# RWKV-7 outputs accumulated channel-major from head-centred values, with the group norm's variance from block-ones products

## The chip, the cores and the metric

The kernel runs on one NeuronCore of a Trainium2 chip. The metric is device time in microseconds (us) of one execution, lower is better; the median of three timed runs stands for the kernel. The profile is of one more execution of the same program.

## The reference, cut to what matters

The model is a two-layer decoder trunk over 1024 tokens of width 1024. The change touches only the RWKV-7 branch of the first layer, which has 16 heads of 64 channels. After its recurrence each head's output is normalised over the head's 64 channels, a bonus is added, and the result is gated and given to the output projection:

```python
def step(state, inp):
    r_t, w_t, k_t, v_t, kk_t, b_t = inp
    sa = -jnp.einsum('bhij,bhj->bhi', state, kk_t)
    state = (state * w_t[:, :, None, :] + sa[..., None] * b_t[:, :, None, :]
             + v_t[..., None] * k_t[:, :, None, :])
    return state, jnp.einsum('bhij,bhj->bhi', state, r_t)
...
mean = jnp.mean(y, -1, keepdims=True)
var = jnp.mean(jnp.square(y - mean), -1, keepdims=True)
y = ((y - mean) * lax.rsqrt(var + RW_GN_EPS)).astype(p.dtype).reshape(b, s, h * n) * ln_w + ln_b
bonus = jnp.sum(r * k * r_k, -1, keepdims=True) * v
return y + bonus.reshape(b, s, h * n)
```

The state's row index is the value's channel, and every term that enters y is linear in v. If v is centred over a head's 64 channels, y comes out centred over them too, so the mean over the head is zero and the variance is the mean of y squared.

## The kernel before

TensorE never runs a stage alone. One long chain of dense products (the projections; rows `mm<-xhi,wh`, `mm<-xlo,wh`, `mm<-xhi,wl` in the trace, three per 128x512 product of exact parts) runs in the background, and the stages are streams (Python generators) with a higher rank. The class `Flow` sets TensorE's order when the program is built: it keeps a planned time, a stream yields what its next step waits for (a planned time, PSUM buffers, an event), and the first ready stream in rank emits its next products; the background chain fills the rest. That order is fixed on TensorE. The order on VectorE, ScalarE and GpSimd comes from the tile framework's own schedule; each of them works strictly in its queue's order.

The RWKV stage lies between about 60 and 1090 us of the span. Its work is cut into 16 units: 8 head pairs times two halves of 512 tokens, each unit four chunks of 128 tokens. Per unit:

- `rw_prep0`, `rw_prep1`: channel-wise work (128 channels = two heads on partitions, 512 tokens). `rw_prep1` transposes V, B and K to token-major (`tok`, by TensorE, copied by ScalarE) and makes the masked products `gr`.
- `rw_inv0`, `rw_inv1`: inverses of triangular blocks. `rw_inv0` has a chain of 62 dependent small operations on GpSimd (L710 and L712, tiles `titmp` and `ti`) with transfers before and after.
- `rw_seq`: the four chunks in turn. Two such streams (of two head pairs) run interleaved. Within a chunk: `rp` and `sp` products, `up` products that give the next state (VectorE, L827, tile `s0c`), and last the outputs, five products into the bank `yps`.
- `rw_out`: group norm, bonus, gate, result to DRAM. Its first part runs when a unit's `rw_seq` has ended; it then yields 10 planned us; its second part begins with four transposes on TensorE.

Before the change the outputs are token-major, and `rw_out` does this: VectorE sums y over each head (L841), subtracts the mean (L844), ScalarE squares (L847), VectorE sums the squares (L848) and finds the inverse root by Newton's method in 15 operations on 128x8 elements (`rsqrt`, L869 to L877, tile `gmv`); **GpSimd multiplies y by it (L850, tile `ty`)**; TensorE transposes `ty` to channel-major (`g<-ident,ty`); VectorE applies weight and bias (L858), adds the bonus (L861) and gates (L862). The five output products of a chunk are these, all in fp32, which the trace shows as two records per product:

```python
F.matmul(yp[:, b, :], lhsT=kr[:, b, 1, :], rhs=sc, start=True, stop=False)
for h, hs in enumerate(hsl):
    F.matmul(yp[:, b, hs], lhsT=gb[:, h, 1, :], rhs=tok[:, 0, b, hs], start=False, stop=False)
    F.matmul(yp[:, b, hs], lhsT=gr[:, b, h, :], rhs=sa[:, h, :], start=False, stop=(h == 1))
```

L179 is the one line through which all matmuls go and L183 the one for transposes, so groups are told apart by their tiles. L404 and L405 split a tile into two exact parts, `hi` by ScalarE and `lo` by VectorE. `head_sums` multiplies two such parts by `blk`, a matrix of ones on the two 64x64 diagonal blocks.

Of the kernel before, what the change touches and what calls it, by code (L numbers as in the profile page):

```python
# [29 lines left out]
# ---------------------------------------------------------------- host layout  # L30
# [24 lines left out]
def host_arrays(inp):  # L55
# [5 lines left out]
    # the S5 channels of a tile: by channel in the group, then by group  # L61
# [26 lines left out]
    # rows 32 r + q, column 2 c + i: channel q of group 2 r + i of tile c  # L88
# [23 lines left out]
    # by head pair, for both halves of the rows  # L112
# [46 lines left out]
class Flow:  # L159
    """The order of TensorE's work. Streams (generators) share it: the first one in rank that is  # L160
    ready goes on by a step. A stream yields what its next step waits for: a time in us from now,
    a PSUM tag and a number of its buffers, the name of an event, or a list of these."""
# [8 lines left out]
    # TensorE, in the order of the calls  # L171
# [13 lines left out]
    # PSUM buffers  # L185
# [11 lines left out]
    # events  # L197
# [27 lines left out]
    def run(self, until):  # L225
        """until the given streams have ended"""
# [19 lines left out]
class Item:  # L246
    """One product of the dense chain: out[m, tokens] = w^T x as three products of exact parts.
    x(h): (hi, lo) [128, kt, 512]; evac(h, psum) takes a half of the tokens. gen: any other work instead"""
# [8 lines left out]
class Tiles(list):  # L257
    """tiles [128, n], indexed as one [128, k, n] would be"""
# [6 lines left out]
class K:  # L265
# [4 lines left out]
    # ------------------------------------------------------------ constants  # L270
    def consts(self, es):
# [22 lines left out]
        # 1 - mu  # L294
# [10 lines left out]
    def new_banks(self, g, yps):  # L305
        """banks besides the dense chain's two"""
# [13 lines left out]
    # ------------------------------------------------------------ dense  # L320
    def load_w(self, parts, src, kt, m=P, pool=None):
        """generator: exact parts of a weight tile [128, kt, m], in pieces; yields the end of each"""
# [14 lines left out]
    def dense(self, items):  # L337
        """generator: the chain of dense products, the weights of the next ones loaded ahead"""
# [17 lines left out]
        def fill(n):  # L356
            """weights of the items up to the next but one, as far as there is room"""
            while at[0] < min(n, len(items) - 1) or live[0] < WB and at[0] < min(n + 2, len(items) - 1):
                at[0] = next(todo)
# [42 lines left out]
    def split(self, hi, lo, src):  # L402
        """hi + lo = src exactly, each with float32r's significand"""
        self.nc.scalar.copy(hi, src)  # L404
        self.nc.vector.tensor_tensor(lo, src, hi.bitcast(F32), A.subtract)  # L405

    def split_load(self, pool, hi, lo, src, n=HT):
        """exact parts of a DRAM tile [128, T]"""
# [5 lines left out]
    def gate2(self, g, ps):  # L414
        """g = 2 * silu(ps)"""
# [4 lines left out]
    def keep_evac(self, kind, dst):  # L420
        """evac of a projection to DRAM: 'gate', 'u' or 'copy'"""
        nc = self.nc

        def evac(h, ps):
            t = self.wp.tile([P, HT], F32, name="ev", bufs=2)
            if kind == "u":
                # tokens by place in the block, last first
# [11 lines left out]
    def put_y(self, kt, s, y):  # L439
        """y [128, n]: out-projection input kt, to DRAM"""  # L440
        self.nc.sync.dma_start(self.yd[kt, :, s], y)

    # ------------------------------------------------------------ norms
    def rstd(self, r, n, fill, scale_mat, rank_wait=0):
        """generator: r [128, n] = (mean over channels + eps)^-1/2 on every partition;
        fill(i, s): squares of one part of the channels for tokens s, or None after the last"""
# [14 lines left out]
    def norm_first(self, p, h, xhi, xlo):  # L461
        """generator: half of the input's tokens as exact parts, first without their norm (a factor per token, self.r0)
        for the products that come first, then with it"""
# [42 lines left out]
    def rw_consts(self, p):  # L506
# [10 lines left out]
        nc.vector.memset(self.p5, 0.5)  # L517
        self.blk = p.tile([P, P], F32R, name="blk")
# [4 lines left out]
        # per channel: w0 / 2, a0 / 2, 1 - k_a  # L523
# [6 lines left out]
        # identity start of the 32-row triangular inverses, in 4 interleaved column groups  # L530
        self.t0 = p.tile([P, 8, 32], F32, name="t0")
        nc.gpsimd.memset(self.t0, 0.0)
        for q in range(4):
            # t - 4 cc - q != 0 keeps 0, else 1
# [1940 lines left out]
```

## Time and profile before

| | |
|---|---|
| timed runs | 2821.52, 2826.01, 2829.27 us; median 2826.01 |
| profiled execution, first to last instruction | 2839.6 us (its time outside the span is not reported) |
| TensorE matmul busy | 2604.9 us, 92% of the span |
| VectorE / ScalarE / GpSimd busy | 1787.5 / 1250.4 / 807.9 us |
| mean granted TensorE clock | 0.944 of 2.4 GHz |

A busy share is an average over stages that have different limits. In this kernel TensorE's order is fixed, so time is lost where TensorE stands idle or runs at the lower clock, and the view that says why is the list of what its instructions waited for. "idle before ... <-" in a row names the idle time of that engine just before the instruction and what ended it.

### The profile page before, as it was taken

The page shows a single profiled execution, that of the slowest core. Times are in us where ns is not written, and L with a number is a line of the kernel's source. Part 1 is how long each engine was busy: PE and PEld are TensorE (multiplying, and loading weights), DVE is VectorE, ACT ScalarE, POOL GpSimd, SP SyncE. Part 2 cuts the span into 40 slices and gives each one's busy share as a digit, 9 for nine tenths or more (in the row PEclk, how much of TensorE's full clock was granted, in tenths as well). Part 3 has the DMA queues.
Part 4 walks back from the last instruction along what each step waited for, and adds up shares of the span by engine and source line. Part 5 has one row for each costly group of instructions (what it writes and reads, how often), then busy time and mean ns, then how long its engine had stood idle before and what let it go on. Part 6 is the DMA issues. An engine that isn't in the chain of part 4 may idle for free.

```text
span 2839.6 us, 42364 instructions
## 1 busy us (share of the span) xinstructions
PE 2604.9 (92%) x15058; PEld 2058.7 (72%) x15058; DVE 1787.5 (63%) x3383; ACT 1250.4 (44%) x2446; POOL 807.9 (28%) x1507
## 2 busy tenths in 40 slices
PE   7998899998998998888999998989899989999998
PEld 5776777776777776675678776767787767777786
DVE  8755556665655537787656457877734887776532
ACT  7433334333443333545533346435434445555443
POOL 4433544345435403354200111251420120000011
PEclk9998989999999989987999999999999999999999
DMA  4332223333232243454584564242455231113643
GB/s 156 115 100 77 84 77 90 95 86 93 85 100 68 70 127 134 107 162 150 160 274 137 162 189 122 79 107 77 113 163 190 88 103 62 44 45 98 197 134 100
DMA packets 263860, 328.27 MB, mean 116 GB/s; under 512 B 88017, under 2 KB 135249, under 8 KB 263137
## 3 DMA queue, kind: packets, MB, share of 16 engines
q1 hardware_dynamic: 260736, 319.39, 37.1%
q0 software_dynamic: 1280, 4.20, 0.4%
q8 instruction: 119, 1.95, 0.3%
q10 hardware_dynamic: 1632, 1.98, 0.2%
q14 instruction: 93, 0.75, 0.1%
HBM read 232.59 MB, written 92.90 MB: 115 GB/s over the span
## 4 chain that ended last, share of the span: by engine, by line
PE 50%; DMA 16%; DVE 15%; POOL 8%; issue 5%; ACT 4%; SPq 1%; DVEq 0%; ACTq 0%; POOLq 0%
PE mm L179 32%; PE g L179 12%; DMA ai<-d_in 5%; PE yps L179 3%; POOL ti L712 3%; POOL titmp L710 3%; PE g L183 2%; DVE wl L405 2%; DMA lm<-acd 1%; DMA gsz<-zd 1%; DMA w<-in_w_ev_out 1%; DMA d_in<-ga 1%; DMA spl<-yg 1%; DMA y<-yt 1%; DMA spl<-yd 1%
## 5 line engine op out<-in xcount | busy, mean ns | idle before, releaser
L405 DVE TENSOR_TENSOR wl<-w,wh 128x512 fp32r<-128x512 f32 (+2 forms) x410 | 285.0, 699 | 295.5 <-ACT wh L404 288.4
L404 ACT CAST wh<-w 128x512 fp32r<-128x512 f32 (+2 forms) x410 | 241.9, 594 | 429.4 <-PE mm L179 274.3
L179 PE MATMUL mm<-xhi,wh 128*128 128x512 f32 x832 | 371.0, 446 | 25.5 <-DVE ev L418 13.7
L179 PE MATMUL mm<-xlo,wh 128*128 128x512 f32 x832 | 344.2, 414 | 4.7 <-DVE xlo L496 2.4
L179 PE MATMUL mm<-xhi,wl 128*128 128x512 f32 x832 | 343.1, 412 | 0.0
L179 PE MATMUL mm<-x1h,wh 128*128 128x512 f32 (+1 forms) x608 | 254.4, 418 | 25.1 <-ACT craw L1822 14.3
L179 PE MATMUL mm<-x1h,wl 128*128 128x512 f32 (+1 forms) x608 | 243.4, 400 | 0.0
L179 PE MATMUL mm<-x1l,wh 128*128 128x512 f32 (+1 forms) x608 | 243.1, 400 | 0.0
L710 POOL TENSOR_TENSOR titmp<-ai,ti 128x60 f32<-128x60 f32 (+24 forms) x496 | 151.3, 305 | 313.8 <-DMA ai<-d_in 277.1
L179 PEld LDWEIGHTS mm<-xhi,wh 128*128 128x128 f32 x832 | 165.6, 199 | 82.7 <-issue 24.2
L179 PEld LDWEIGHTS mm<-xhi,wl 128*128 128x128 f32 x832 | 165.4, 199 | 40.5
L179 PEld LDWEIGHTS mm<-xlo,wh 128*128 128x128 f32 x832 | 166.6, 200 | 36.2 <-DVE xlo L474 5.0
L712 POOL TENSOR_TENSOR ti<-ti,titmp 128x60 f32<-128x60 f32 (+24 forms) x496 | 161.2, 325 | 38.2
L179 PEld LDWEIGHTS mm<-x1h,wh 128*128 128x128 f32 (+1 forms) x608 | 117.9, 194 | 59.0 <-ACT craw L1822 17.3
L179 PEld LDWEIGHTS mm<-x1l,wh 128*128 128x128 f32 (+1 forms) x608 | 117.6, 193 | 27.6 <-issue 3.6
L179 PEld LDWEIGHTS mm<-x1h,wl 128*128 128x128 f32 (+1 forms) x608 | 117.2, 193 | 27.0
L179 PE MATMUL mm<-yb,wh 128*128 128x512 f32 x320 | 102.4, 400 | 5.8 <-ACT yb L404 4.5
L785 DVE TENSOR_TENSOR gb<-g,m 128x256 f32<-128x256 f32 x128 | 49.5, 419 | 73.2 <-PE g L179 73.0
L799 ACT ACTIVATE sn<-s0c,fin 64x64 f32<-64x64 f32 x128 | 44.1, 345 | 106.4 <-DVE s0c L827 57.8
L1673 POOL TENSOR_TENSOR sq<-sq,sqt 128x512 f32<-128x512 f32 x14 | 18.0, 1289 | 245.7 <-DMA w<-in_w_ev_out 161.0
L2266 POOL CAST pth<-zero 128x128 fp32r<-128x128 f32 x32 | 11.3, 353 | 241.4 <-PE yps L179 179.8
L418 DVE SCALAR_TENSOR_TENSOR ev<-ev,mm 128x512 f32<-128x512 f32 x72 | 49.1, 682 | 45.5 <-ACT ev L417 45.2
(598 smaller groups left out, 6612.7 us busy)
## 6 DMA issues: line engine op xcount, KB each, us to landing
w<-in_w_ev_in SPq DMA_DIRECT2D x106, 256.0 KB
w<-in_w_od_in SPq DMA_DIRECT2D x82, 256.0 KB
w<-in_w_ev_out SPq DMA_DIRECT2D x64, 256.0 KB
w<-in_w_od_out SPq DMA_DIRECT2D x64, 256.0 KB
rd<-ev SPq DMA_DIRECT2D x50, 256.0 KB
spl<-yd SPq DMA_DIRECT2D x40, 256.0 KB
zod<-ev SPq DMA_DIRECT2D x36, 256.0 KB
ai<-d_in SPq DMA_DIRECT2D x16, 512.0 KB
```

What stands on the lines that cost most here:

```text
L179: return self._pe(self.nc.tensor.matmul(out, lhsT=lhsT, rhs=rhs, start=start, stop=stop, **kw), math.prod(rhs.shape[1:]), rhs.dtype)
L183: return self._pe(self.nc.tensor.transpose(out, src, ident), src.shape[0] // 2, F32)
L404: self.nc.scalar.copy(hi, src)
L405: self.nc.vector.tensor_tensor(lo, src, hi.bitcast(F32), A.subtract)
L418: nc.vector.scalar_tensor_tensor(g, g, 1.0, ps, A.add, A.mult)
L710: eng.tensor_tensor(tm, ai[:, s:s + 1, s + 1:32].broadcast_to([P, n, w]), ti[:, 0:n, s:s + 1].broadcast_to([P, n, w]), A.mult)
L712: eng.tensor_tensor(ti[:, 0:n, s + 1:32], ti[:, 0:n, s + 1:32], tm, A.subtract)
L785: nc.vector.tensor_tensor(gb[:, h], pgs[h], self.m2, A.mult)
L799: nc.scalar.mul(sg[hs], sc[hs, hs], g[hs])
L1673: nc.gpsimd.tensor_tensor(self.sq1, self.sq1, t, A.add)
L2266: nc.gpsimd.tensor_copy(t[:, n, 0:P], self.zero)
```

## The change

It does five things, all within the RWKV stage; the other lines of the full diff remove comments and docstrings, so line numbers shift by a few.

1. V, when copied from PSUM to `tok[:, 0]`, is centred over each head: a reduction and a fused multiply-add on VectorE take the place of ScalarE's copy.
2. The output products swap operands, so y comes out channel-major: four products with 64 weight columns and 128 moving columns, whose outputs go to the lower and the upper 64 partitions in turn, then one with 128 weight columns.
3. `rw_out` loses the means, the Newton iterations, GpSimd's multiplication and the four transposes. The variance is a `head_sums` product of y squared, in two exact parts; the inverse root is Ln and Exp on ScalarE.
4. y and its square are kept in the unit's `gr` tile, so that tile is held until `rw_out` has read it.
5. The load of the gate (`sz`) comes after `head_sums`, whose `lo` part is in the same buffer.

```diff
@@ rw_consts
+        self.epsg = p.tile([P, 1], F32, name="epsg")
+        nc.vector.memset(self.epsg, 64e-5)
@@ rw_prep1
-            nc.scalar.copy(tok[:, i], tp)
-            F.rel("g", 2.0)
+            if i:
+                nc.scalar.copy(tok[:, i], tp)
+                F.rel("g", 2.0)
+            else:
+                h8 = lambda ap: ap.rearrange("p b (h i) -> p (b h) i", h=2)
+                mv = wk.tile([P, 8], F32, name="vmean", bufs=2)
+                nc.vector.tensor_reduce(mv, h8(tp), AX.X, A.add)
+                nc.vector.scalar_tensor_tensor(h8(tok[:, 0]), mv.unsqueeze(2).broadcast_to([P, 8, 64]), -1.0 / 64,
+                                               h8(tp), A.mult, A.add)
+                F.rel("g", 3.0)
@@ rw_seq
-            F.matmul(yp[:, b, :], lhsT=kr[:, b, 1, :], rhs=sc, start=True, stop=False)
             for h, hs in enumerate(hsl):
-                F.matmul(yp[:, b, hs], lhsT=gb[:, h, 1, :], rhs=tok[:, 0, b, hs], start=False, stop=False)
-                F.matmul(yp[:, b, hs], lhsT=gr[:, b, h, :], rhs=sa[:, h, :], start=False, stop=(h == 1))
+                F.matmul(yp[hs, b, :], lhsT=tok[:, 0, b, hs], rhs=gb[:, h, 1, :], start=True, stop=False)
+            for h, hs in enumerate(hsl):
+                F.matmul(yp[hs, b, :], lhsT=sa[:, h, :], rhs=gr[:, b, h, :], start=False, stop=False)
+            F.matmul(yp[:, b, :], lhsT=sc, rhs=kr[:, b, 1, :], start=False, stop=True)
@@ rw_out (the part before it, and rsqrt, are removed)
+        g = st["gr"].rearrange("p b h t -> p (b h t)")
+        y, r = g[:, 0:HT], g[:, HT:]
+        nc.scalar.copy(y, yp)
+        nc.scalar.square(r, yp)
         F.rel("yps", 3.0)
+        parts = t("ty", F32R), t("sz", F32R)
+        self.split(*parts, r)
+        yield [9.0, ("g", 1)]
+        ps = self.bank("g")
+        self.head_sums(ps, parts)
+        sz, o = t("sz"), t("ty")
         nc.sync.dma_start(sz, zd[p, :, s])
+        nc.scalar.activation(r, ps, AF.Ln, scale=1.0 / 64, bias=self.epsg)
+        F.rel("g", 3.5)
+        nc.scalar.activation(r, r, AF.Exp, scale=-0.5)
+        stt = nc.vector.scalar_tensor_tensor
+        stt(o, y, self.col("rw_ln_w", p), r, A.mult, A.mult)
+        stt(o, o, self.col("rw_ln_b", p), st["bon"], A.add, A.add)
+        stt(o, o, 0.5, sz, A.mult, A.mult)
```

The order moves in three places that matter below. On TensorE, before, in the last chunk of the first unit and behind it (`yps` is the output bank, `ident,ty` the transposes of `rw_out`):

```order
L179 MATMUL yps<-s0c_582,kr 128x128
L179 MATMUL yps<-tok,gb_1986 128x64
L179 MATMUL yps<-sa_2096,gr 128x64
...
L179 MATMUL g<-tok,gb_2189 128x64 x2
L179 MATMUL g<-s0c_586,kr 128x128
L179 MATMUL mm<-xhi,wh 128x512
L179 MATMUL mm<-xlo,wh 128x512
L179 MATMUL mm<-xhi,wl 128x512
L183 MATMUL g<-ident,ty 128x128 x4
```

On TensorE after the change, at the same place (the `yps` rows shown are those of the other stream's chunk that follows):

```order
L179 MATMUL yps<-gb_2107,tok 64x128 x2
L179 MATMUL yps<-gr,sa_2173 64x128 x2
L179 MATMUL yps<-kr,s0c_586 128x128
...
L179 MATMUL g<-kr,tg 128x128 x8
L179 MATMUL g<-tok,gb_2175 128x64 x2
L179 MATMUL g<-s0c_588,kr 128x128
L179 MATMUL g<-ty,blk 128x512
L179 MATMUL g<-sz,blk 128x512
```

The two `head_sums` products stand where the four transposes stood. Over the whole program fewer background products are emitted inside the RWKV stage: 2154 `mm` products stand ahead of the last output product before, 2118 after; the other 36 follow later, and from the end of the S5 stage on TensorE's order is the same in both.

On GpSimd before, in the first unit; `titmp` and `ti` are another unit's inverse chain:

```order
L712 TENSOR_TENSOR ti<-ti,titmp 128x7x7
L710 TENSOR_TENSOR titmp<-ai,ti 128x7x6
L850 TENSOR_TENSOR ty<-ty,gmv 128x512
L712 TENSOR_TENSOR ti<-ti,titmp 128x7x6
L710 TENSOR_TENSOR titmp<-ai,ti 128x7x5
```

`rw_out`'s multiplication stands deep inside that chain. After the change no operation of `rw_out` is on GpSimd.

On VectorE, in the fifth unit, before (L655 masks `gr`; L827 makes the next chunk's state; L858 is the first operation of `rw_out` behind the transposes):

```order
L565 SCALAR_TENSOR_TENSOR ev<-mm,cols,ev 128x511
L655 TENSOR_TENSOR gr<-g,m_540 128x4x128 x2
L827 SCALAR_TENSOR_TENSOR s0c_586<-g,fin,sn_4576 64x64 x2
L858 TENSOR_SCALAR ty<-g,cols 128x512
L405 TENSOR_TENSOR cc<-tb,ce 128x512
```

And on VectorE after the change, in the same unit (L869 is the first operation behind Exp; L657 masks `gr`, L838 makes the state):

```order
L796 TENSOR_TENSOR gb_4522<-g,m_540 128x256 x2
L869 SCALAR_TENSOR_TENSOR ty<-gr,cols 128x512
L870 SCALAR_TENSOR_TENSOR ty<-ty,cols,bon 128x512
L657 TENSOR_TENSOR gr<-g,m_540 128x4x128 x2
L838 SCALAR_TENSOR_TENSOR s0c_588<-g,fin,sn_4487 64x64 x2
```

The state update, which stood ahead of the operation that waits, now stands behind it; it does so directly in three of the 16 units.

## Rows read from the trace of the kernel before

**Rows 1.** The page's first part: busy us (share of the span) x instructions

```profile
PE 2604.9 (92%) x15058; PEld 2058.7 (72%) x15058; DVE 1787.5 (63%) x3383; ACT 1250.4 (44%) x2446; POOL 807.9 (28%) x1507
```

**Rows 2.** Windows view: length, then PE, PEld, DVE, ACT, POOL busy; clock; DMA

```profile
60.00:1090.00 1030.00, 955.58 (x6843) 751.94 (x6842) 602.43 (x1357) 391.07 (x825) 426.13 (x1144) 0.93 0.31 91
```

**Rows 3.** Waits of TensorE, 60 to 1090 us: total us, times, longest

```profile
PE g L183 <- POOL ty L850: 43.2, 13, 7.4
PE g L179 <- DVE xn L727: 11.7, 11, 3.1
PE g L179 <- DVE tg L622: 7.9, 3, 5.9
```

**Rows 4.** Timeline around the first wait: start, us, engine, line, operation [idle before]

```profile
219.91 0.17 DVE L877 TENSOR_TENSOR gmv<-gmv 128x8 f32<-128x8 f32 x1
...
231.03 1.04 POOL L850 TENSOR_TENSOR ty<-ty,gmv 128x512 f32<-128x512 f32 x1
...
232.12 1.11 PE L183 MATMUL g<-ident,ty 128*128 128x128 f32 x4 [7.40 <-POOL ty L850]
```

**Rows 5.** Windows view, eight stretches at the lower clock: the first, and their sum

```profile
226.40:236.60 10.20, 4.48 (x16) 3.79 (x16) 3.22 (x5) 0.02 (x1) 7.93 (x25) 0.50 0.00 0
...
sum 47.60, PE 32.73 PEld 27.13 DVE 23.93 ACT 1.87 POOL 39.72; mean PE 4.09 PEld 3.39 DVE 2.99 ACT 0.23 POOL 4.97
```

**Rows 6.** Timeline of TensorE, one chunk of the first unit, full clock

```profile
207.80 0.70 PE L179 MATMUL g<-kr,km 64*128 64x256 f32 x4
208.44 0.50 PE L179 MATMUL mm<-xhi,wh 128*128 128x512 f32 x1
...
209.24 0.39 PE L179 MATMUL mm<-xhi,wh 128*128 128x512 f32 x1
...
210.02 0.34 PE L179 MATMUL g<-tok 128*64 128x64 f32 x4
...
210.41 0.49 PE L179 MATMUL yps<-s0c,kr 128*128 128x128 f32 x2
210.74 0.33 PE L179 MATMUL yps<-tok,gb 128*128 128x64 f32 x2
...
211.57 0.61 PE L179 MATMUL g<-tok,gb 128*128 128x64 f32 x4
212.02 0.44 PE L179 MATMUL g<-s0c,kr 128*128 128x128 f32 x2
212.22 0.48 PE L179 MATMUL mm<-xhi,wh 128*128 128x512 f32 x1
```

**Rows 7.** Timeline of TensorE: four transposes, and a pair of head sums

```profile
217.72 0.60 PE L183 MATMUL g<-ident,rv 128*128 128x128 f32 x4
218.16 0.60 PE L183 MATMUL g<-ident,tg 128*128 128x128 f32 x4
...
220.21 0.48 PE L179 MATMUL g<-ce,blk 128*128 128x512 f32 x1
...
220.76 0.60 PE L183 MATMUL g<-ident,km 128*128 128x128 f32 x4
```

**Rows 8.** Timeline of ScalarE in the odd layer: Ln and Exp of a norm

```profile
1948.63 1.28 ACT L457 ACT_TABLE_LOAD   x1
1949.92 0.69 ACT L457 ACTIVATE mr<-g,eps 128x512 f32<-128x512 f32 x1
...
1951.92 0.63 ACT L459 ACTIVATE mr<-mr 128x512 f32<-128x512 f32 x1
```

**Rows 9.** VectorE by line, 60 to 1090 us: count | busy us, mean ns | idle before, releasers

```profile
L827 DVE SCALAR_TENSOR_TENSOR s0c<-g,fin,sn 64x64 f32<-64x64 f32 x96 | 27.0, 281 | 19.4 <-PE g L179 18.5
L858 DVE TENSOR_SCALAR ty<-g,cols 128x512 f32<-128x512 f32 x16 | 13.0, 810 | 54.0 <-PE g L183 38.4 <-POOL titmp L710 12.0 <-POOL ti L712 3.6
L861 DVE TENSOR_TENSOR ty<-ty,bon 128x512 f32<-128x512 f32 x16 | 11.8, 739 | 0.2
```

**Rows 10.** Timeline of VectorE: the two masked copies of `gr`

```profile
223.38 1.29 DVE L655 TENSOR_TENSOR gr<-g,m 128x512 f32<-128x512 f32 x2
```

More of the change, by code (lines that the diff above doesn't have):

```diff
@@ L837, in rw_out @@
         s = slice(hh * HT, (hh + 1) * HT)
-        yp = st["yp"].rearrange("p b (h i) -> p (b h) i", h=2)
-        b8 = lambda ap: ap.unsqueeze(2).broadcast_to([P, 8, 64])
-        mv = wk.tile([P, 4, 8], F32, name="gmv", bufs=1)
-        nc.vector.tensor_reduce(mv[:, 0], yp, AX.X, A.add)
-        nc.vector.tensor_scalar(mv[:, 0], mv[:, 0], 1.0 / 64, None, A.mult)
-        y = wk.tile([P, 8, 64], F32, name="ty", bufs=1)
-        nc.vector.tensor_tensor(y, yp, b8(mv[:, 0]), A.subtract)
-        F.rel("yps", 3.0)
@@ L846, in rw_out @@
-        sq = wk.tile([P, 8, 64], F32, name="sz", bufs=1)
-        nc.scalar.square(sq, y)
-        nc.vector.tensor_reduce(mv[:, 1], sq, AX.X, A.add)
-        self.rsqrt(mv[:, 1], mv[:, 1], mv[:, 2:4], 1.0 / 64, 64e-5)
-        nc.gpsimd.tensor_tensor(y, y, b8(mv[:, 1]), A.mult)
-        sz = wk.tile([P, HT], F32, name="sz", bufs=1)
-        nc.sync.dma_start(sz, zd[p, :, s])
-        yield [10.0, ("g", 1)]
-        tp = self.bank("g", (P, 4, P))
-        for b in range(4):
-            F.transpose(tp[:, b, :], y[:, 2 * b:2 * b + 2].rearrange("p h i -> p (h i)"), self.ident)
@@ L857, in rw_out @@
-        o = wk.tile([P, HT], F32, name="ty", bufs=1)
-        nc.vector.tensor_scalar(o, tp.rearrange("p b t -> p (b t)"), self.col("rw_ln_w", p), self.col("rw_ln_b", p),
-                                A.mult, A.add)
-        F.rel("g", 1.2)
-        nc.vector.tensor_tensor(o, o, st["bon"], A.add)
-        nc.vector.scalar_tensor_tensor(o, o, 0.5, sz, A.mult, A.mult)
-        self.put_y(p, s, o)
-    def rsqrt(self, out, x, tmp, scale, eps):
-        v = self.nc.vector
-        h, t = tmp[:, 0], tmp[:, 1]
-        v.tensor_scalar(h, x, scale, eps, A.mult, A.add)
-        i = lambda ap: ap.bitcast(I32)
-        v.tensor_scalar(i(t), i(h), 1, None, A.logical_shift_right)
-        v.tensor_scalar(i(out), i(t), -1, 0x5f3759df, A.mult, A.add)
-        for _ in range(3):
-            v.tensor_tensor(t, out, out, A.mult)
-            v.tensor_tensor(t, t, h, A.mult)
-            v.tensor_scalar(t, t, -0.5, 1.5, A.mult, A.add)
-            v.tensor_tensor(out, out, t, A.mult)
+        yp = st["yp"].rearrange("p b t -> p (b t)")
@@ new lines, in rw_out @@
+        t = lambda n, dt=F32: wk.tile([P, HT], dt, name=n, bufs=1)
+        g = st["gr"].rearrange("p b h t -> p (b h t)")
+        y, r = g[:, 0:HT], g[:, HT:]
+        nc.scalar.copy(y, yp)
+        nc.scalar.square(r, yp)
+        F.rel("yps", 3.0)
+        parts = t("ty", F32R), t("sz", F32R)
[4 more added lines that the diff above has]
+        sz, o = t("sz"), t("ty")
+        nc.sync.dma_start(sz, zd[p, :, s])
```

## The prediction

> **What bounds the kernel now.** I read the page first: TensorE is busy 92% of the span, VectorE 63%, ScalarE 44%, GpSimd 28% [rows 1]. TensorE's order is fixed when the program is built, so a microsecond counts only where TensorE stands idle, works slowly, or has fewer products to do. The windows view of the RWKV stage gives the room: of 1030 us TensorE is busy 955.6 at a mean clock of 0.93, while VectorE has 602 us of work, ScalarE 391 and GpSimd 426 [rows 2]. None of these three is short of time; what they can be is late. TensorE is idle 1030.0 - 955.6 = 74.4 us there, and the list of its waits says for what: 43.2 us in 13 waits go to one operation, GpSimd's multiplication `ty`, with the transposes waiting behind it; the next is `xn` with 11.7 us [rows 3]. All other waits make up 74.4 - 43.2 = 31.2 us.
>
> The timeline shows why. In the first unit VectorE ends Newton's method at 219.91 + 0.17 = 220.1 us, and GpSimd starts the multiplication only at 231.0, though it needs 1.04 us. It stands in GpSimd's queue behind the operations of another unit's inverse chain. TensorE has used up the products that stand ahead of the transposes and is idle 7.40 us [rows 4]. The reader is to see that the wait is a place in a queue, not a duration.
>
> The waits cost a second time. Eight of the 13 are followed by, or end in, a stretch in which the granted clock is 0.50, so 1.2 instead of 2.4 GHz. The eight last 47.6 us, and TensorE is busy 32.7 us of them [rows 5]. At the full clock that work takes half, so 16.4 us were lost.
>
> **The change part by part.** I sum against the profiled execution, whose span of 2839.6 us is 13.6 us (0.5%) above the median of the timed runs; the differences are taken off the median, 2826.0.
>
> *The wait for GpSimd goes: -43.2 us, and its slow stretches: -16.4 us.* TensorE's next wait at that place is for the head sums' `lo` part: ScalarE copies, squares and rounds, VectorE subtracts. Three ScalarE operations near the 0.63 us of a 128x512 Exp [rows 8] and a subtraction near 0.74 [rows 9] make 2.6 us. The planner puts 9 us of products between; the queues ahead may hold 6 us more work and nothing is lost. VectorE also no longer stands 54.0 us before L858 [rows 9], so it serves all other streams sooner.
>
> *Output products: -20 us.* A chunk's five took 210.41 to 211.57 = 1.16 us [rows 6], and there are 64 chunks. The new ones have no row, so I bound them. From below: the four state products of 128x64 weights, two heads going to two halves of the partitions, took 0.39 us to the next product, and one product with 128 columns each way 0.20 (212.02 to 212.22) [rows 6]: 0.59 us, 64 x 0.57 = 36 us saved. From above: each of the five takes what the first output product took, 0.33 us (210.41 to 210.74) [rows 6]: 1.65 us, 31 us lost. I take a row with the same number of moving columns: `km` products, two side by side with 256 columns each, took 0.64 us (207.80 to 208.44) [rows 6]. Four of 128 columns, two side by side, move as much, and with 0.20 for the last one a chunk takes 0.84, so 0.32 x 64 = 20 us are saved. What the rows show is that with 64 columns and full weights a product costs no less than one with 128: in the old chunk ten records came every 0.11 us. There are ten records after, eight of them with half the weights.
>
> The Trainium skill speaks against this term: "FP8 and Floating Point Precision", section "TensorE Precision Notes", has true fp32 as four passes through the array, so cost would go with moving columns, 4 x 64 + 128 = 384 before and 5 x 128 = 640 after. By that the outputs would be dearer by 256 x 4 / 2.4 GHz = 0.43 us a chunk, 27 us in all, an estimate from that page. The trace agrees only for 128 columns (0.20 us); for 64 columns the product took as long, so the old form did not get its cheap columns.
>
> *Transposes out, head sums in: +2 us.* Four transposes took 0.44 us (217.72 to 218.16), a pair of head sums 0.55 (220.21 to 220.76) [rows 7]; 16 x 0.11 = 1.8 us.
>
> *VectorE, ScalarE, GpSimd.* VectorE loses two sums, a subtraction, Newton's 15 small operations and a bias, and gets a sum and a fused operation for V and a subtraction: less work on an engine with 428 us to spare [rows 2]. GpSimd loses its multiplication. ScalarE gets, per unit, five operations and two table loads, about 3 x 0.63 + 0.69 + 0.63 + 2 x 1.28 = 5.8 us [rows 8], and loses two copies like them, some 1.2: 16 x 4.6 = 74 us on top of 391 of 1030 [rows 2]. I cost that at nothing, covered by ScalarE's free half; if the cover is gone it is the first rival.
>
> *36 background products move behind the RWKV stage.* They are 8 us of work that is done later, so nothing in the sum. They change which products stand beside the S5 stage's work; 10 us either way in the range.
>
> *What is late next: +16 us.* TensorE reaches everything else (43.2 + 16.4 + 20) / 16 = 5 us earlier per unit, while the inverse chain and VectorE keep their pace. The other 31.2 us of waits should grow. Nothing in the trace shows by how much: zero from below, doubling from above. I take half again, 16 us.
>
> Sum: 43.2 + 16.4 + 20 - 1.8 - 16 = 62 us, and 2826 - 62 = **2764 us**.
>
> **Rivals.**
>
> *ScalarE's Ln and Exp hold up the recurrence, and it is slower.* Behind the head sums stand Ln 0.69, a table load 1.28 and Exp 0.63 [rows 8], then on VectorE two operations of 0.74 [rows 9], the two masks of `gr`, 1.29 [rows 10], and in three units the state update directly behind them, two of 0.28 [rows 9]: 5.9 us. TensorE's products ahead of the one that needs that state are, in the fifth unit, five background triples at up to 0.80 (208.44 to 209.24), four state products, 0.39 [rows 6], an output group, 0.84, and ten small products: some 6 us, so the path is just covered. Against the rival: it is direct in three units only, and the old L858 stood 54.0 us idle without holding TensorE as long. For it: no slack is left, and the tile `gr` is now held until that path has ended. It becomes slower where the new waits w with their slow stretches (16.4 per 43.2, so a factor 1.38) eat the gain before new waits, 78: 16 x 1.38 x w > 78, so w > 3.5 us in every unit. With 5 us it costs 110: 2826 - 78 + 110 = 2858 us. Chance 0.07.
>
> By "ScalarE: Activation LUTs", section "What ACT_TABLE_LOAD costs", of the Trainium skill a switch of tables costs about 1.38 us of drain on top of the load of 1.283. The trace has the load but no drain: Ln starts 0.01 us after its load ends. With the drain twice the path would be 2.8 us longer, in three units, some 8 us in all.
>
> *The output products get no cheaper or dearer.* Their halves of the array would not work side by side. Unchanged gives 2784, the upper bound 2764 + 20 + 31 = 2815 us. For it: the first output product took 0.33 us, not 0.20, when TensorE came from 64-column weights [rows 6]. Against it: the state products took 0.39 for four. Chance 0.15.
>
> *The wait only moves.* GpSimd's inverse chain, which the multiplication waited behind, is as long as before; `xn` and `tg` waits [rows 3] would take what `ty` gave up. If they double the rest (31 us instead of 16) and give back half of the clock (8): 2764 + 15 + 8 = 2787; if all of `ty` reappears there, only the products' gain is left: 2826 - 18 = 2808 us. Chance 0.13; a further 0.05 that nothing moves beyond what this kernel's measurement can tell, 0.3% or 8.5 us.
>
> **How the numbers follow.** The forecast has 0.60, with its own range of 2740 to 2786: waits of 0 to 31 us and S5 10 us either way. From below, the cheapest output products, no new wait and a lucky S5 stage give 2826 - 43 - 16 - 36 + 2 - 10 = 2723. From above the range takes in unchanged output products with doubled waits, 2784 + 16 = 2800. So 2723 to 2802, which leaves out most of the slow rival, the upper end of the other two and little below: 2 in 10. Faster has 0.60 + 0.15 + 0.13, same 0.05, slower 0.07.
>
> **What would show it.** No wait for a GpSimd `ty` and TensorE idle below 55 us in the RWKV stage; a clock near 0.95 there; output groups of 0.6 to 0.85 us a chunk; the last output product some 55 to 75 us earlier; `xn` or `tg` waits a little longer; the odd layer as before. The prediction is wrong if output groups take over 1.16 us, if waits for ScalarE's `rh` or `sa` or VectorE's `s0c` or `gr` of several us stand in most units, or if the S5 stage gets longer by more than the 8 us that moved into it.

## The result, and the profile after

The changed kernel is slower, not faster: 2844.87 us against 2822.3 us for the kernel before, medians of 20 runs each on one chip; the ratio is 1.0068, 95% interval 1.0053 to 1.0083. On a second chip it came to 1.004 (1.0021 to 1.006; `after_again` below). The profiled execution has a span of 2846.0 us, 6.4 above that of before, and a mean granted clock of 0.942. Single executions of either kernel differ by up to 0.9% (before 2815.43 to 2839.52 us), so sizes are taken from the ratios, and the profiles are used for where time goes. The odd layer shows what one profile can hide: behind the second mark (below), where TensorE's order is the same in both, it took 1360.6 us before and 1345.2 after.

The page's busy times and the windows view of the RWKV stage, after (they answer to [rows 1, 2]):

```profile
PE 2586.2 (91%) x15026; PEld 2017.8 (71%) x15026; DVE 1751.1 (62%) x3128; ACT 1330.8 (47%) x2533; POOL 785.8 (28%) x1491
```

```profile
60.00:1090.00 1030.00, 940.51 (x6826) 715.42 (x6825) 568.56 (x1109) 461.70 (x911) 416.50 (x1136) 0.93 0.31 93
684.50:697.00 12.50, 9.13 (x38) 6.21 (x39) 5.16 (x10) 3.55 (x6) 10.15 (x31) 0.73 0.18 60
988.90:1012.40 23.50, 6.39 (x97) 5.04 (x98) 3.67 (x6) 6.19 (x14) 3.78 (x3) 0.56 0.42 113
```

All engines but ScalarE have less work, as the change promises, and TensorE is idle longer in the same 1030 us: 1030 - 940.5 = 89.5 us, where it was 74.4. The list of TensorE's waits in that stretch, after (answers to [rows 3]), says for what:

```profile
PE g L179 <- DVE xn L738: 29.7, 9, 16.5
PE g L179 <- DVE tg L624: 13.9, 6, 5.1
PE g L179 <- ACT sa L825: 10.3, 9, 2.5
PE g L179 <- ACT gr L865: 7.0, 14, 1.0
PE g L179 <- DVE gb L796: 6.9, 4, 2.4
...
PE g L179 <- DVE gr L657: 3.4, 6, 0.9
PE g L179 <- DVE s0c L838: 2.9, 4, 1.6
```

The wait for `ty`, 43.2 us, is gone. In its place stand many small ones that were not there, and `xn` and `tg` are 24 us longer. One unit's end shows the small ones. Timeline of after, all engines, lines left out:

```profile
682.32 0.50 PE L179 MATMUL g<-ty,blk 128*128 128x512 f32 x1 [0.39 <-ACT sa L825]
...
683.47 1.28 ACT L865 ACT_TABLE_LOAD   x1
...
684.77 0.69 ACT L865 ACTIVATE gr<-g,epsg 128x512 f32<-128x512 f32 x1
...
685.47 1.28 ACT L867 ACT_TABLE_LOAD   x1
...
685.51 0.70 PE L179 MATMUL g<-kr,km 64*128 64x256 f32 x2 [1.04 <-ACT gr L865]
...
686.76 0.63 ACT L867 ACTIVATE gr<-gr 128x512 f32<-128x512 f32 x1
...
687.43 0.75 DVE L869 SCALAR_TENSOR_TENSOR ty<-gr,cols 128x512 f32<-128x512 f32 x1 [3.25 <-ACT gr L867]
...
688.10 0.42 DVE L796 TENSOR_TENSOR gb<-g,m 128x256 f32<-128x256 f32 x1
...
688.57 1.22 PE L179 MATMUL g<-kr,km 64*128 64x256 f32 x2 [2.37 <-DVE gb L796]
```

The head sums' bank is free only when Ln (L865) has read it, and Ln stands behind a table load: TensorE waits 1.04 us. Then VectorE stands 3.25 us before L869, which wants the Exp behind the second table load; `gb` is queued behind L869, and TensorE waits 2.37 us for a product that has nothing to do with the output. The stretch from 684.5 has a granted clock of 0.73.

The longest wait is a chain of queues near the stage's end. Timeline of after, all engines:

```profile
997.95 0.63 ACT L1014 ACTIVATE macc<-mraw 128x512 f32<-128x512 f32 x1 [19.14 <-DMA mraw<-in_memT]
...
1003.06 0.60 ACT L404 CAST wh<-w 128x512 fp32r<-128x512 f32 x1
...
1003.69 1.35 DVE L405 TENSOR_TENSOR wl<-w,wh 128x512 fp32r<-128x512 f32 x1 [20.53 <-ACT wh L404]
1004.96 1.36 DVE L738 STREAM_TRANSPOSE xn<-xt 32x256 f32<-32x256 f32 x3
...
1005.44 0.31 PE L179 MATMUL g<-xn,ga 32*32 32x32 f32 x2 [16.49 <-DVE xn L738]
```

ScalarE waits for the load of the memory input (`mem_norm`, nothing of RWKV), the weight's cast `wh` is behind it, VectorE's `wl` needs `wh`, and `xn` is behind `wl`. From 988.9 to 1012.4 TensorE has 6.4 us of work in 23.5, and its clock is 0.56.

The output products did get cheaper. TensorE's timeline in the last chunk of one stream, after (answers to [rows 6]):

```profile
982.35 0.40 PE L179 MATMUL yps<-gb,tok 128*64 128x128 f32 x4
982.57 0.40 PE L179 MATMUL yps<-gr,sa 128*64 128x128 f32 x4
982.89 0.49 PE L179 MATMUL yps<-kr,s0c 128*128 128x128 f32 x2
983.14 0.48 PE L179 MATMUL mm<-xhi,wh 128*128 128x512 f32 x1
```

From 982.35 to 983.14 is 0.79 us, where the old five took 1.16. Counted over all chunks in the two traces, the middle values are 0.79 and 1.15 us.

**Two marks split the program.** The background chain has the same order in every kernel here, so when the first `mm<-yh,wh` starts (output projection of RWKV's y, while the S5 stage ends), the same background work and all of RWKV are done, but not the same part of S5. The first `mm<-gh,wh` comes when S5 is done too, so only the second mark stands behind equal work. The view groups TensorE's instructions by tile, with "first to last start". Before:

```profile
L179 PE MATMUL mm<-yh,wh x128: 388/394/793, 1285.4 to 1478.3; 128*128 128x512 f32 x128
L179 PE MATMUL mm<-gh,wh x128: 388/389/501, 1479.0 to 1567.2; 128*128 128x512 f32 x128
```

After:

```profile
L179 PE MATMUL mm<-yh,wh x128: 388/398/797, 1285.1 to 1500.1; 128*128 128x512 f32 x128
L179 PE MATMUL mm<-gh,wh x128: 389/389/397, 1500.8 to 1587.2; 128*128 128x512 f32 x128
```

At the first mark the two are level (1285.4, 1285.1), though I had the last output product alone 55 to 75 us earlier; it came 11 us earlier (1075.1, 1064.0). The loss shows between the marks: 193.6 us before, 215.7 after, though fewer of TensorE's products besides the background are left to do there (counted in the traces, 560 before and 496 after, beside 384 of the background in both). The windows view of that stretch, before and after:

```profile
1285.40:1479.00 193.60, 175.05 (x948) 130.80 (x945) 125.69 (x213) 94.03 (x198) 46.79 (x40) 0.92 0.61 188
1285.10:1500.80 215.70, 186.90 (x883) 138.06 (x881) 120.21 (x208) 99.61 (x202) 41.65 (x40) 0.84 0.59 185
```

Of the 22 us, 10 are idle time (28.8 against 18.6) and 12 are slower work, at a granted clock of 0.84 where it was 0.92. TensorE waits there for the two parts of the reloaded y, in after (first two rows of its waits from 1285.1 to 1500.8):

```profile
PE mm L179 <- ACT yh L404: 11.5, 4, 3.6
PE mm L179 <- DVE yl L405: 9.2, 6, 3.6
```

Before, the same two rows are 0.8 and 3.9 us.

### The profile page after: what moved, and what is told of

It reads as the page before. It is cut to its first block, busy times and chain, and to the rows that moved or that the text cites. A ratio compares the mean times of both kernels' runs of the same rounds, so it can differ in the third digit from the quotient of the medians.

```text
span 2846.0 us, 42087 instructions
## 1 busy us (share of the span) xinstructions
PE 2586.2 (91%) x15026; PEld 2017.8 (71%) x15026; DVE 1751.1 (62%) x3128; ACT 1330.8 (47%) x2533; POOL 785.8 (28%) x1491
## 5 line engine op out<-in xcount | busy, mean ns | idle before, releaser
L721 POOL TENSOR_TENSOR titmp<-ai,ti 128x60 f32<-128x60 f32 (+24 forms) x496 | 159.8, 322 | 298.9 <-DMA ai<-d_in 261.5
L810 ACT ACTIVATE sn<-s0c,fin 64x64 f32<-64x64 f32 x128 | 44.1, 345 | 97.2 <-DVE s0c L838 78.4
L179 PE MATMUL g<-kr,km 64*128 64x256 f32 x256 | 56.2, 450 | 23.2 <-ACT sa L825 8.8
```

The source lines that it names most:

```text
L179: return self._pe(self.nc.tensor.matmul(out, lhsT=lhsT, rhs=rhs, start=start, stop=stop, **kw), math.prod(rhs.shape[1:]), rhs.dtype)
L721: eng.tensor_tensor(tm, ai[:, s:s + 1, s + 1:32].broadcast_to([P, n, w]), ti[:, 0:n, s:s + 1].broadcast_to([P, n, w]), A.mult)
L810: nc.scalar.mul(sg[hs], sc[hs, hs], g[hs])
```

## The experiments

Three theories came out of the profile. Theory 1: the path head sums, Ln, Exp, VectorE holds TensorE up in every unit. Theory 2: the one stall near 989 us. Theory 3: the S5 stage has other products beside it, since the plan moved some there. Every ratio is against the kernel before on the same chip, with its 95% interval; the chips differ between groups of runs. `before_prod`, `before_ty_prod`, `before_ty`, `charge_notab` and `noln_charge` rest on 4 to 7 executions, the others on 9 to 20. "First mark" and "second mark" are as above, from one profile each.

| kernel | ratio (95% interval) | first mark, us | second mark, us |
|---|---|---|---|
| before | 1 | 1285.4 | 1479.0 |
| after (result) | 1.0068 (1.0053 to 1.0083) | 1285.1 | 1500.8 |
| `after_again` | 1.0040 (1.0021 to 1.0060) | 1285.6 | 1499.3 |
| `notab` | 1.0010 (0.9990 to 1.0030) | 1267.5 | 1476.1 |
| `late_ve` | 1.0003 (0.9983 to 1.0024) | 1262.3 | 1479.3 |
| `memlate` | 1.0015 (0.9994 to 1.0035) | 1275.9 | 1465.3 |
| `before_memlate` | 1.0011 (0.9993 to 1.0029) | 1285.2 | 1477.4 |
| `late_mem` | 0.9981 (0.9966 to 0.9996) | 1256.7 | 1466.8 |
| `own` | 0.9992 (0.9968 to 1.0015) | 1270.8 | 1481.4 |
| `before_ty` | 0.9876 (0.9851 to 0.9902) | 1250.3 | 1444.8 |
| `before_prod` | 0.9908 (0.9894 to 0.9922) | 1259.9 | 1448.4 |
| `before_ty_prod` | 0.9827 (0.9789 to 0.9865) | 1242.2 | 1428.2 |
| `before_prod_over` | 1.0055 (1.0029 to 1.0081) | 1304.1 | 1492.1 |
| `charge` | 0.9939 (0.9914 to 0.9963) | 1240.6 | 1457.9 |
| `own_late_mem_charge` | 0.9943 (0.9917 to 0.9968) | 1228.4 | 1456.4 |
| `charge_notab` | 0.9914 (0.9885 to 0.9942) | 1229.9 | 1447.9 |
| `noln_charge` | 1.0079 (1.0051 to 1.0106) | 1270.9 | 1489.5 |
| `charge_low` | 0.9931 (0.9906 to 0.9956) | 1230.2 | 1455.7 |
| `charge_mid` | 0.9991 (0.9973 to 1.0008) | 1259.5 | 1472.6 |
| `charge_mid_own` | 0.9976 (0.9955 to 0.9997) | 1246.6 | 1463.6 |

**The waits seen in the profile, one repair each.**

```diff
# notab
-        nc.scalar.activation(r, ps, AF.Ln, scale=1.0 / 64, bias=self.epsg)
+        nc.scalar.activation(r, ps, AF.Identity, scale=1.0 / 64, bias=self.epsg)
-        nc.scalar.activation(r, r, AF.Exp, scale=-0.5)
+        nc.scalar.activation(r, r, AF.Identity, scale=-0.5)
# late_ve, behind Exp
+        yield 6.0
-        stt(o, y, self.col("rw_ln_w", p), r, A.mult, A.mult)
+        F.tc.keep_in_program_order(stt(o, y, self.col("rw_ln_w", p), r, A.mult, A.mult))
# memlate and before_memlate, mem_norm, behind the load
+        yield 25.0
-                nc.scalar.square(acc, raw[:, 0:2])
+                self.flow.tc.keep_in_program_order(nc.scalar.square(acc, raw[:, 0:2]))
```

`notab`: 

> The changed kernel with the Ln and the Exp of the output's inverse root replaced by two Identity operations of the same size, so ScalarE has no table load there (this leaves out the inverse root); every other instruction keeps its place on its engine. Theory 1 (the path head sums, table load, Ln, table load, Exp, then VectorE holds TensorE up in every unit): the path is 2.6 us shorter, so of the 29 us of waits for Ln, sa, gb, gr and s0c some 20 go, with their slow stretches about 28 us: near 2817. Theory 2 (one stall near 989 us, behind ScalarE's wait for the memory input): no change, 2845. Theory 3 (the S5 stage's neighbours): no change, 2845.

`late_ve`: 

> The changed kernel with VectorE's three last operations of an output issued 6 planned us after Exp and the first of them pinned behind what VectorE was given before, so that gb and gr no longer stand behind an operation that waits for Exp; the table loads stay. Theory 1: the waits for gb, gr and s0c (13 us) go, and their slow stretches, about 18 us: near 2827; the waits for Ln and sa stay. If the table loads alone matter: 2840 to 2845. Theories 2 and 3: 2845, give or take 6 for the shift of the products around.

`memlate`: 

> The changed kernel with ScalarE's first square of the memory input issued 25 planned us after its load and pinned behind what ScalarE was given before. Theory 2: the 16.5 us wait for xn near 989 us goes, and the 20 us at half the clock behind it, which cost 10: near 2820. Theories 1 and 3: no change beyond 5 us, 2845.

`before_memlate`: 

> The same edit in the kernel before. Theory 2: its wait at that place is 4.9 us, so it gains 5 to 8 us, 2815, and the changed kernel's loss against it shrinks from 22 to about 5. If the edit acts by something else than that wait, both kernels gain alike.

The three ratios of the changed kernel are 0.3 to 0.6% below its 1.0040 and 1.0068, less than forecast, and none is below 1; their intervals overlap that of `after_again`, so no single one of these gains is certain. The table loads are real: without them, and with no other instruction moved, TensorE's waits for Ln are gone and those for `sa` fall from 10.3 to 3.8 us. Its waits in `notab` from 60 to 1090:

```profile
PE g L179 <- DVE xn L738: 33.1, 16, 16.2
...
PE g L179 <- DVE s0c L838: 13.1, 3, 7.7
...
PE g L179 <- ACT sa L825: 3.8, 9, 0.8
PE g L179 <- DVE gb L796: 3.3, 4, 0.9
```

`xn` and `s0c` took up 14 us of what went. `late_ve` does what it is for on VectorE, which stands idle before L869 for 1.5 us in all, where it was 44.1. But TensorE's waits for `gb`, `gr` and `s0c` fall only from 13.2 to 11.5 us.

`memlate` does not do what it is for. Only the first square of the memory input was moved; the second (L1018) then stood ahead of it in ScalarE's queue and waited for the same load. Timeline of `memlate`:

```profile
993.17 0.63 ACT L1018 ACTIVATE mt<-mraw 128x512 f32<-128x512 f32 x1 [18.53 <-DMA mraw<-in_memT]
...
996.64 0.31 PE L179 MATMUL g<-xn,ga 32*32 32x32 f32 x2 [11.85 <-DVE xn L738]
```

TensorE's wait there fell from 16.5 to 11.9 us instead of to nothing, and `late_mem` and `own_late_mem_charge`, with the same edit, have ScalarE idle there for 12.9 and 13.8 us. So theory 2 is not tested by these runs. In `before_memlate` the wait of 4.9 us that TensorE had is gone, and the time is the same (1.0011). Theory 1 is a part at most, since without the table loads the kernel is still no faster than before; what the stall costs stays open.

`late_mem`, both edits: 

> The changed kernel with both edits, VectorE's last output operations behind gb and the square of the memory input later. Theories 1 and 2 together: the two gains of 0.65% and 0.53% add, ratio 0.995 against the kernel before. If each only uncovers the next wait: no better than either alone, 1.000 to 1.002.

The ratio of 0.9981 is between the two readings. On this chip the changed kernel has 1.0040 (`after_again`, below), so the two edits together give 0.6%, with the stall shorter, 9.7 us, but not gone.

`own`, in which y and the inverse root no longer stand in `gr` (the square still does, until its low part is formed; the constant `t0` becomes bfloat16 for the room):

```diff
-        y, r = g[:, 0:HT], g[:, HT:]
+        y, r = t("yown"), g[:, HT:]
         sz, o = t("sz"), t("ty")
+        r = o
```

> The changed kernel with y in a tile of its own and the inverse root in the output's tile, so that the unit's gr is free as soon as the low part of the square is formed; room is made by a constant in bfloat16. TensorE's order is the same row for row. If the held gr costs (its masks and gb stand behind the output's end): 0.3 to 0.6% better than the changed kernel, ratio 0.998 to 1.001. If not: 1.004, as the changed kernel has.

It gave 0.9992 with TensorE's order untouched: the held tile seems to cost some 0.5% too, by ratios from different chips. `after_again`, on the chip of `late_mem`: 

> The changed kernel as it is, beside the others on the same chip: ratio 1.007 as in the result, 1.004 to 1.010.

**The two gains by themselves.** If so many things each cost half a per cent, something makes TensorE sensitive to all of them. So the kernel before was given the gains alone.

```diff
# before_ty
-        nc.gpsimd.tensor_tensor(y, y, b8(mv[:, 1]), A.mult)
+        nc.vector.tensor_tensor(y, y, b8(mv[:, 1]), A.mult)
# before_prod: the five new output products, and behind them
+            F.now -= 4 * 64 * 4 / 2400
```

`before_ty`: 

> The kernel before with the multiplication ty on VectorE in place of GpSimd, and nothing else; TensorE's order is the same row for row. If the removed wait is worth what the prediction took for it (43 us and 16 us of slow stretches, less some 16 for what is late next): 1.5% faster, ratio 0.985. If what stands behind it in the inverse chain and the S5 stage takes the gain back, as it did in the changed kernel: ratio 0.993 to 1.000.

`before_prod`: 

> The kernel before with the five output products of the changed kernel in place of its own, charged to the planner like the old ones; the rest of the output's work reads the bank as if it were still token-major, so the output's values are not the reference's. If the products are cheaper by the 23 us that the profile after shows for their group and TensorE bounds: ratio 0.992. If a gain before a fixed wait only lengthens that wait (ty, then the S5 stage): 0.998 to 1.001.

`before_ty_prod`: 

> The kernel before with both parts that gain by themselves, ty on VectorE and the new output products with the old charge (the output's values are not the reference's, since the rest reads the bank as token-major). If the gains add: 0.9876 x 0.9908, ratio 0.979, 60 us, which is the prediction's sum before new waits. If a bound behind them takes part of it back: 0.983 to 0.988.

Both are there: 1.24% of 2839 us is 35 us (28 to 42), 0.92% is 26 (22 to 30), and together 1.73% or 49 us (38 to 60), where the two singly make 61; the intervals do not keep these apart. (The 60 us are called the prediction's sum before new waits above; that sum is 78, and 62 is the one after them.) `before_ty` is an edit of one word and the fastest kernel here that computes everything. In it TensorE's waits move on, but are fewer; from 60 to 1090:

```profile
PE g L179 <- ACT rh L807: 25.0, 6, 7.9
PE g L179 <- DVE xn L727: 14.4, 16, 3.2
PE g L179 <- DVE tg L622: 9.8, 3, 6.8
```

**The plan's price.** `Flow._pe` charges an fp32 product four planned cycles per moving column. For a chunk's outputs that was (128 + 4 x 64) x 4 / 2400 = 0.64 planned us, and is now 5 x 128 x 4 / 2400 = 1.07, while on the chip they fell from 1.16 to 0.79. `before_prod` gives the difference of 0.43 back, so that the plan is as before. `before_prod_over` is the same kernel without that line. `charge` is the changed kernel with it.

`before_prod_over`: 

> The kernel before with the new output products at the changed kernel's price in the plan (1.07 planned us a chunk; the output's values are not the reference's). If the price alone costs, because the plan then puts fewer background products between dependent steps while the chip is faster than before: it loses 0.7 to 1.2% against the same products at the old price, ratio 0.998 to 1.003. If the plan's price only mattered together with the Ln-Exp path: 0.991, as with the old price.

`charge`: 

> The changed kernel, in which the planner is charged for a chunk's output products as for the old ones (0.64 planned us instead of 1.07), so that about as many background products stand in the RWKV stage as before. If the plan's shift (36 products moved into the S5 stage, fewer of them beside the recurrence) is the missing cost: ratio 0.985 to 0.995 against the kernel before. If the Ln-Exp path and the held gr are: 1.004, as the changed kernel has on this chip, give or take 0.003.

This settles one large part. The same products at the old price have 0.9908, at the new one 1.0055: the price alone costs 1.5%, some 42 us. In the changed kernel the old price gives back 1.0 to 1.3% (0.9939 against 1.0040 and 1.0068), 28 to 37 us, and makes it faster than the kernel before. The windows view up to the second mark, so over the same work, and the waits of the RWKV stage, with the old price (`before_prod`):

```profile
60.00:1448.40 1388.40, 1237.58 (x8825) 963.40 (x8825) 889.98 (x1761) 577.91 (x1195) 561.61 (x1261) 0.93 0.39 115
```

```profile
PE g L183 <- POOL ty L852: 57.0, 13, 8.3
PE g L179 <- DVE xn L727: 15.2, 15, 3.4
PE g L179 <- DVE tg L622: 9.5, 3, 5.5
```

and with the new price (`before_prod_over`):

```profile
60.00:1492.10 1432.10, 1252.52 (x8825) 972.83 (x8824) 895.52 (x1762) 581.45 (x1198) 558.21 (x1261) 0.92 0.37 112
```

```profile
PE g L183 <- POOL ty L851: 70.0, 14, 9.2
PE g L179 <- DVE xn L727: 18.9, 16, 7.2
PE g L179 <- DVE tg L622: 11.3, 4, 5.5
PE g L179 <- ACT sa L814: 6.4, 1, 6.4
```

Counted in the traces, 1731 background products stand between the first and the last output product at the old price, and 1656 at the new one. Every delay in the plan (`H`, `HA`, `HV` and the rest) is in planned us. A dearer price fills these delays with fewer products, on a chip that runs the outputs faster than before, and TensorE comes too early to what others still have to make. The second mark says how much: 1448.4 against 1492.1, 44 us. Of these, 29 are idle time (150.8 and 179.6 us) and 15 are slower work, at a mean clock of 0.93 and 0.92.

**What is left at the old price.**

`own_late_mem_charge`: 

> The changed kernel with all four repairs: y in its own tile, VectorE's last output operations behind gb, the square of the memory input later, the old charge. If the changed kernel's loss is made of these: between the 0.979 of its two gains and 0.99. If the table loads are the larger part, which stay here: 0.995 to 1.000.

`charge_notab`: 

> The changed kernel with the old price in the plan and two Identity operations in place of Ln and Exp, which leaves out the inverse root and with it the table loads. If the table loads are what is left of the loss: ratio 0.983 to 0.988. If they cost nothing once the plan gives cover: 0.994, as with the loads.

`noln_charge`, the inverse root by a guess and two steps (`epsg` holds the guess's constant, and the sum's bank is free after the first line):

```diff
+        v.tensor_scalar(r, ps, 1.0 / 64, 64e-5, A.mult, A.add)
+        nc.scalar.activation(o, r.bitcast(I32), AF.Exp, scale=-0.5 * math.log(2) / 2 ** 23, bias=self.epsg)
+        for _ in range(2):
+            v.tensor_tensor(u, o, o, A.mult)
+            stt(u, u, -0.5, r, A.mult, A.mult)
+            stt(o, u, 1.5, o, A.add, A.mult)
```

> The changed kernel with the old price in the plan and the inverse root without Ln: a first guess by one Exp of the bits, then two steps of Newton's method, seven operations of 128x512 on VectorE, no table load. If the table loads are what is left: 0.983 to 0.990, less what 4 us more of VectorE's work per unit costs. If VectorE's order is: worse than 0.994.

With the price put right, `own` and `late_mem` give nothing more (0.9943 against 0.9939), and the table loads 0.25%, which these intervals can't tell from none. The Newton path costs 1.4% against `charge`: TensorE then waits for what ScalarE and VectorE have queued. Its waits in `noln_charge` from 60 to 1090:

```profile
PE g L179 <- ACT sa L825: 18.8, 11, 11.5
PE g L179 <- DVE xn L738: 18.6, 14, 7.3
PE g L179 <- DVE gb L796: 16.6, 9, 10.8
```

At the first mark `charge` (1240.6) is as early as `before_ty_prod` (1242.2), but that is not equal work: `charge` still has 680 products besides the background ahead of its second mark, `before_ty_prod` 560. At the second mark it is 30 us later (1457.9, 1428.2), and by the ratios, both from one chip, 1.1% or 32 us slower. So the rest of the change, put in place of the old `rw_out` with `ty` on VectorE, costs that much at the old price, and the repairs above give back little or none of it. Two more prices looked for the reason.

`charge_low`, twice the amount given back: 

> The changed kernel with a price of 0.21 planned us a chunk, less than the old one, so that still more background products stand in the RWKV stage. If more cover there is still worth something: 0.988 to 0.992. If the stall then moves to the S5 stage, which loses its cover: 0.994 to 1.000.

`charge_mid`, 0.30 given back: 

> The changed kernel with 0.77 planned us for a chunk's output products (0.30 less than it has), the price at which as many background products stand in the RWKV stage as before (1731), and 453 beside the S5 work (450 before). If the S5 stage loses because its neighbours are others: it loses nothing here against the kernel before, and the ratio is 0.985 to 0.990. If the S5 loss comes with the RWKV stage's earlier end whatever stands beside it: 0.993 to 0.998, as at the other prices.

`charge_mid_own`: 

> The same with y in a tile of its own, so that gr is not held; TensorE's order is that of charge_mid row for row. If the held gr costs beside the price: 0.3 to 0.6% better than charge_mid. If it only showed because TensorE ran ahead of its plan: the same as charge_mid within 0.2%.

`charge_mid` has before's count of background products in each stage, and still took 213.1 us between the marks: the count is not the reason, and theory 3 in that form falls. Its ratio of 0.9991 is above both readings, the second of which its interval just reaches. Its first mark comes 19 us after that of `charge`, with 120 more of the other products done; at the second mark 15 us are left, though only 30 background products differ in the RWKV stage.

The four prices put the changed kernel in order: with 1.07, 0.77, 0.64 and 0.21 planned us the second mark comes at 1500.8, 1472.6, 1457.9 and 1455.7. Below the old price there is little left to gain. A price changes not only how many background products stand between dependent steps but also which; no run separates the two. The ratios of `charge_mid` and `charge_mid_own` overlap, so what `gr` costs there is not told apart.

**What stays open.** In the six profiles with the old `rw_out` the stretch between the marks takes 186.0 to 194.5 us; in 13 of the 14 with the new one 208 to 228, and 189.4 in `memlate`. In `after` TensorE waits there for `yh` and `yl`, and ScalarE's cast `yh` for the load of y: 11.9 us, where `before_ty_prod` has 1.0 and `memlate` 5.8. The amount of work in the stretch does not explain it: `late_ve`, `memlate`, `late_mem` and `charge_mid` have 560 products besides the background there, like before, and took 217.0, 189.4, 210.1 and 213.1 us. Why y comes late with the new outputs, and less so in `memlate`, no run tells; it is worth some 20 to 30 us.

## Why the prediction was wrong, by its steps

The forecast was 62 us faster, and the kernel is 11 to 19 us slower. The runs part the difference into three. The two gains in the kernel before give 49 us instead of 62 (`before_ty_prod`). The rest of the change at the old price takes 32 of these (`charge`, 17 us faster than before). The new price takes another 28 to 37. Of the second part the size is known and not the cause; that of the third is the step named below as failed.

- **The wait for GpSimd, -43.2 and -16.4: right in kind, too large.** No `ty` wait is left, and `before_ty` has it as a gain of 35 us by itself (28 to 42). With its share of the new waits, 16 x 59.6 / 79.6 = 12, I had 48; `rh`, `xn` and others took about 24 of the 59.6 us back.
- **Output products, -20: right.** 0.79 us a chunk against 0.84 forecast, and 26 us by themselves. The rival in which they are no cheaper falls. By the Trainium skill ("FP8 and Floating Point Precision", section "TensorE Precision Notes"), read as a cost per moving column summed over the products, they would have been dearer; the trace does not agree for these shapes, where 640 columns took 0.79 us and 384 took 1.16. The plan's price is such a sum.
- **36 background products move behind the RWKV stage, "nothing in the sum": this step failed.** I counted them as work done elsewhere. They were what stood between dependent steps, and the cause that moved them, the price, was in front of me as 5 x 128 against 128 + 4 x 64 columns. It costs 42 us in `before_prod_over`, where 75 such products move and nothing else of the change is there but the output products, and 28 to 37 us in the changed kernel.
- **What is late next, +16: mis-sized.** The idle time besides `ty` went from 31.2 to 89.5 us, so 58 where I had 16 and, at the most, 31. The price is not the whole reason: at the old one (`charge`) the same 1030 us still have 1030 - 943.2 = 86.9 us of idle time:

```profile
60.00:1090.00 1030.00, 943.15 (x6903) 718.94 (x6901) 581.94 (x1123) 467.95 (x923) 427.44 (x1142) 0.95 0.33 97
```

- **ScalarE's and VectorE's new work at nothing: this step failed too.** With the centring of V and the held `gr` it is the rest of the change, which costs 32 us at the old price. Table loads, the place of L869 and the held `gr` seem to cost 0.3 to 0.6% each in the changed kernel, and at the old price no more than the runs can tell apart; what the 32 us are made of stays open. That ScalarE and VectorE are idle much of the time did not cover a late operation: what stands behind it in its queue, as `gb` behind L869, waits too.
- **The S5 stage, 10 either way: mis-sized.** The stretch between the marks is 22 us longer; open, see above. It was among my own signs of being wrong. (By the terms named for it, the forecast's range is 2738 to 2789, not 2740 to 2786.)

Of the rivals, the ScalarE one named the right side and the right path, with another victim: `gb` and the bank behind Ln, not the state. The loads in it are not the main cause, since `notab` still has 1.001. The rival in which waits move to `xn` and `tg` happened as well: 19.6 us became 43.6, of which 16.5 are the one stall at the memory input. That a TensorE ahead of its plan makes both is my reading; at the old price `xn` and `tg` still have 34.8 us.

## What to carry to other kernels

Where a planner interleaves background work by its own clock, a change to an operation is also a change to its price there: work out the planned duration before and after beside the real one, and if they move apart, keep the old price or set a measured one, then test it alone. Small waits for many different operations, none of which gives much when it is removed, can point to a common cause upstream, here in part cover that is too short. Measure each half of a change by itself in the kernel before: that told in three runs that both gains were real, and so that the loss was in the rest of the change or in how they had been put in. And look in the trace of a repair whether the wait that it was for is gone: in `memlate` it was not. A mark in time compares two kernels only where the same work stands ahead of it.

## What was not expected of the hardware

The two table loads per unit need 2 x 1.28 us of ScalarE's time, and in the timeline above Ln starts 0.02 us after the first (683.47 + 1.28 = 684.75, 684.77), so each costs its own length. More surprising is how far one operation that waits for a load reaches: with it at the head of ScalarE's queue TensorE stood for 16.5 us, and in the 23.5 us around that, with 6.4 us of work, had a mean granted clock of 0.56.
